# Reading the gate and up sums three weight chunks later, and turning units a block later, in an expert stage

## The chip, the cores and the metric

One core of a Trainium2 chip. The time is device microseconds of one launch, first to last instruction of the program on that core. TensorE is called PE (its weight loads PEld), VectorE DVE, ScalarE ACT, GpSimd POOL, SyncE SP; SP issues the transfers.

## The reference

Two transformer blocks on 256 tokens of width 1024, all in float32. The change is in the second block's last part, a mixture of eight experts of which each token takes two:

```python
gates = jnp.sum(jax.nn.one_hot(top_idx, N_EXPERTS) * top_w[..., None], axis=-2)
for e in range(N_EXPERTS):      # h: 256 x 1024; wg, wu: 1024 x 3584; wd: 3584 x 1024
    out = out + gates[..., e:e + 1] * ((jax.nn.silu(h @ wg[e]) * (h @ wu[e])) @ wd[e])
```

## The kernel before

**Precision.** Float32 products are made of rounded halves: `split` (L373) lets ACT cast a value to a short float (the high half, L374) and DVE subtract that from the value (the low half, a `tensor_tensor`, recorded at L339). `mm3` (L446) then makes three matmuls: high by high, high by low, low by high. Every weight is split on the chip.

**Weights.** They come in chunks of 512 rows by 512 columns (1 MB), fetched by SP into a ring of raw buffers (`fetch`, L390). `chunk` (L418) splits a chunk in two steps of 1024 columns, so a chunk is two casts on ACT and two subtractions on DVE. Low and high halves lie in rings of six buffers each in this stage, two per chunk: a chunk's split needs the buffers of the chunk three before it, and so waits until PE has read those. SP fetches into a raw buffer when DVE's subtraction has released it.

**Experts.** They are put in an order by load. Four of the eight are small (up to 64 tokens), four large (up to 128). A large expert keeps the halves of its tokens in separate columns and uses `mm3`; a small one holds both halves side by side in one 128 wide operand and needs two matmuls where a large one needs three. `gather` and `gather_small` collect an expert's tokens by matmuls into a PSUM bank, ACT scales them from there; `scatter` brings results back; `place` prepares both.

**Blocks.** An expert's 3584 columns are seven blocks of 512. A block is six chunks: two for gate (1024 rows), two for up, two for down. The loop over `steps` in `moe` (L2054) first does four blocks of a large expert, then alternates one block of a small and one of a large expert (a pair), and ends with four small ones. The unit that a block makes (silu(gate) times up, turned so that its columns lie on partitions, and split) is multiplied by the down weights in the next step, so that the order of chunks is: gate, gate, up, up of this block, then down, down of the block before.

**Around the sums.** `up` (L2105) takes two PSUM banks of pool `pd`, makes the gate sum in one and the up sum in the other, and lets ACT read the gate sum in between (a large block: Silu into `g`, right behind the splits of the second gate chunk) or at the end (a small block: copy, L2128). `up_end` (L2138 for a small block's up sum, `tt` for a large one's product) reads the up sum behind the first down chunk's splits, and PE turns the result into a bank of pool `ps` at once. `end`, which splits the turned unit into `hu` (L2160 for a large block; Silu, product, cast and subtraction for a small one), is put into `mids[0]`, which the next block's `up` runs after its first gate chunk. `mids` are four lists of such work, one after each chunk of `up`; gathers, scatters and `place` go into lists 1 and 2. The pool `ps` has five banks here, four of them hold the down sums of the two experts in work, and `pd` three.

The order on each engine is the program's order as far as the language's scheduler leaves it; `issue_after(x)` puts what follows behind `x` on its engine.

Of the kernel before, what the change touches and what calls it, by code (L numbers as in the profile page):

```python
# [212 lines left out]
class K:  # L213
# [1840 lines left out]
    def moe(self, x, lg, rs):  # L2054
        A, nc = self.A, self.nc
# [13 lines left out]
        NE, NB = 8, 7  # L2069
        small = [r >= SMALL for r in SEQ]  # L2070
# [31 lines left out]

        def up(e, cb, mids):  # L2105
            XH, XL = state[e][1][0], state[e][1][-1]
            g, ps = self.med(), []
            for nm in ("moe_w_gate_2", "moe_w_up_2"):
                p = self.take("pd")
                ps.append(p)  # L2110
                for kh in (0, 4):
                    with self.scope():
                        args = (W(nm, e), kh * 128, 4, cb * 512, 512)
                        c = self.chunk(*args)
                        for k in range(4):
                            ks = slice((kh + k) * 128, (kh + k) * 128 + 128)
                            if small[e]:
                                for i in range(2):
                                    self.last_mm = self.mm(p, XH[:, ks], c[k][i], kh + k + i == 0, kh + k + i == 8, True)
                            else:  # L2120
                                self.mm3(p, XH[:, ks], XL[:, ks], c[k][0], c[k][1], kh + k == 0, kh + k == 7)
                    for f in mids.pop(0):
                        f()
                if not small[e] and nm == "moe_w_gate_2":
                    self.act(g, p, AF.Silu)
            if small[e]:
                with self.tc.issue_after(self.last_hi.ins):
                    nc.scalar.copy(g, ps[0])  # L2128
            return g, p


        def up_end(e, g, pu):
            hu = self.take("r", 0)
            p = self.take("ps", 0)
            if small[e]:
                gu = self.med()
                with self.tc.issue_after(self.last_hi.ins):
                    nc.scalar.copy(gu, pu)  # L2138
                for i, a in enumerate((g, gu)):
                    for k in range(4):  # L2140
                        self.mm(p[:, i * 256 + k * 64 : i * 256 + k * 64 + 64], a[:, k * 128 : k * 128 + 128], self.cst("ident2"))

                def end():
                    with self.scope():
                        h = self.med()
                        self.act(h[:, :256], p[:, :256], AF.Silu)
                        self.tt(h[:, 256:], p[:, 256:], h[:, :256], ALU.mult)
                        v = hu[:, :512].rearrange("p (k h s) -> p k h s", k=4, h=2)
                        self.split(h[:, 256:].rearrange("p (k s) -> p k s", k=4), v[:, :, 0], v[:, :, 1])
                    self.free(p)  # L2150
                return hu, end
            with self.scope():
                h = self.med()
                self.tt(h, pu, g, ALU.mult)
                for k in range(4):
                    self.tr(p[:, k * 128 : k * 128 + 128], h[:, k * 128 : k * 128 + 128])

            def end():
                with self.tc.issue_after(self.last_hi.ins):
                    self.last_hi = nc.scalar.copy(hu[:, :512], p)  # L2160
                with self.tc.issue_after(self.last_lo.ins):
                    self.tt(hu[:, 512:], p, hu[:, :512].bitcast(F32), ALU.subtract)
                self.free(p)
            return hu, end

        def down(e, cb, hu, half):
            hh, hl = hu[:, :512], hu[:, 512:]
            if cb == half == 0:
                state[e][2] = [self.take("ps", 0), self.take("ps", 0)]
            acc = state[e][2]  # L2170
            with self.scope():
                c = self.chunk(W("moe_w_down_2", e), cb * 512, 4, half * 512, 512)
                for k in range(4):
                    ks = slice(k * 128, k * 128 + 128)
                    first, last = cb == 0 and k == 0, cb == NB - 1 and k == 3
                    if small[e]:
                        self.mm(acc[half], hh[:, ks], c[k][0], first, False)
                        self.last_mm = self.mm(acc[half], hh[:, ks], c[k][1], False, last)
                    else:
                        self.mm3(acc[half], hh[:, ks], hl[:, ks], c[k][0], c[k][1], first, last)  # L2180
            if half:
                self.free(hu)
# [18 lines left out]
        prev, mids = None, [[] for _ in range(4)]  # L2201
        for e, cb in steps:
            with self.scope():
                gp = up(e, cb, mids)
                mids = [[] for _ in range(4)]
                if cb == NB - 1:
                    self.free(*state[e][1])
                if prev:
                    down(*prev, 0)
                hu, end = up_end(e, *gp)  # L2210
                mids[0].append(end)
            if prev:
                for i, f in zip((1, 2), down(*prev, 1) or []):
                    mids[i].append(f)
            prev = (e, cb, hu)
# [24 lines left out]
            f()  # L2240
        for half in range(2):
            self.presplit(W("moe_w_down_2", NE - 1), (NB - 1) * 512, 4, half * 512, 512)
        self.q["pd"].append(self.q["ps"].popleft())
        self.overflow(x, gate, pos, scaled, ad, add, PP[0], cap)
        down(*prev, 0)
        for f in down(*prev, 1):
            f()
        for t in range(2):
            with self.scope():
                r = self.rms_of(t)  # L2250
# [62 lines left out]
```

## Time and profile before

| | |
|---|---|
| runs shown | 2153.07, 2149.79, 2152.31 us, median 2152.31 |
| profiled execution | 2151.22 us, its span 2149.4 us |
| PE busy | 2066.2 us, 96% of the span |
| DVE busy | 1841.5 us, 86% |
| ACT busy | 1325.3 us, 62% |
| read from HBM | 606.75 MB |

Matmuls overlap in the pipeline and their ends are modelled, so a busy PE need not be at its limit. What a wait costs is read from the stretch in which it lies: an engine's idle time is given with what ended it, and idle time of an engine that nothing waits for costs nothing.

### The profile page before, as it was taken

How to read it: one execution, taken by the hardware profiler on the slowest of the kernel's cores; microseconds unless marked ns; L12 is line 12 of the kernel's file. 1: busy time of each engine (PE TensorE's matmuls, PEld its weight loads, DVE VectorE, ACT ScalarE, POOL GpSimd, SP SyncE). 2: the span in 40 equal slices, each digit the busy share in tenths (PEclk: the TensorE clock that was granted, in tenths of full speed). 3: DMA queues.
4: the chain of work that ended last, by engine and by line, in shares of the span. 5: the costliest groups of instructions: out<-in, count | busy, mean ns of one | idle time of the engine just before them, and what ended most of it. 6: DMA issues, size and time to landing. Idle time of an engine off the chain costs nothing. (4 is left out here: it accounts for less than half of the span.)

```text
span 2149.4 us, 31135 instructions
## 1 busy us (share of the span) xinstructions
PE 2066.2 (96%) x11593; PEld 1706.1 (79%) x11593; DVE 1841.5 (86%) x2669; ACT 1325.3 (62%) x1857; POOL 2.1 (0%) x6
## 2 busy tenths in 40 slices
PE   6999999999999999999999999999999999999997
PEld 5987888889988878998997887777777777777765
DVE  6888985898888868888787999998998899998997
ACT  4544354454445435444765887777787778777775
POOL 0000000000000000000000000000000000000000
PEclk9999999999999999999999999999999999999997
DMA  7546767878843527885465899998999899998993
GB/s 306 192 165 214 264 219 255 298 296 303 302 160 117 150 100 262 310 342 212 139 253 188 329 400 368 356 387 321 391 343 377 348 365 377 355 383 322 386 371 140
DMA packets 99997, 610.70 MB, mean 284 GB/s; under 512 B 19156, under 2 KB 24061, under 8 KB 27773
## 3 DMA queue, kind: packets, MB, share of 16 engines
q1 hardware_dynamic: 99836, 608.64, 75.7%
q8 instruction: 92, 1.51, 0.3%
q14 instruction: 69, 0.56, 0.1%
HBM read 606.75 MB, written 3.42 MB: 284 GB/s over the span
## 5 line engine op out<-in xcount | busy, mean ns | idle before, releaser
L354 PE MATMUL pd<-k 128*128 128x512 f32 (+2 forms) x7408 | 1447.2, 349 | 37.8 <-DVE k L339 26.6
L339 DVE TENSOR_TENSOR k<-k,k 128x1024 fp32r<-128x1024 f32 (+2 forms) x1149 | 1229.8, 1112 | 184.4 <-ACT k L374 180.9
L354 PEld LDWEIGHTS pd<-k 128*128 128x128 f32 (+1 forms) x7408 | 1139.1, 190 | 269.3 <-DVE k L339 104.0
L374 ACT CAST k<-k 128x1024 fp32r<-128x1024 f32 (+2 forms) x1131 | 1039.6, 977 | 362.9 <-PE pd L354 184.6
L354 PE MATMUL ps<-k 128*128 128x512 f32 (+8 forms) x3031 | 576.2, 343 | 13.4 <-DVE k L339 3.8
L354 PEld LDWEIGHTS ps<-k 128*128 128x128 f32 (+4 forms) x3031 | 431.6, 179 | 112.1 <-DVE k L339 18.2
L348 DVE SCALAR_TENSOR_TENSOR k<-k,k 128x512 f32<-128x512 f32 (+1 forms) x257 | 188.3, 735 | 2.1 <-ACT k L351 0.2
L351 ACT ACTIVATE k<-pd 128x256 f32<-128x256 f32 (+1 forms) x125 | 57.2, 481 | 101.4 <-PE pd L354 98.5
L351 ACT ACTIVATE k<-k 128x256 f32<-128x256 f32 (+8 forms) x142 | 69.0, 500 | 79.3 <-DVE k L339 41.7
L339 DVE TENSOR_TENSOR k<-k 128x512 f32<-128x512 f32 (+13 forms) x277 | 93.6, 355 | 17.3 <-ACT k L351 12.4
L354 PEld LDWEIGHTS ps<-k,k 128*128 128x128 f32 x526 | 77.0, 199 | 12.4 <-DVE k L348 3.4
L339 DVE TENSOR_TENSOR k<-ps,k 128x512 fp32r<-128x512 f32 (+5 forms) x99 | 56.8, 579 | 24.8 <-PE ps L354 8.7
L354 PE MATMUL ps<-k,k 128*128 128x64 f32 (+3 forms) x526 | 75.0, 269 | 2.9 <-DVE k L348 2.9
L357 PE MATMUL ps<-k,k 128*128 128x128 f32 (+1 forms) x396 | 60.8, 278 | 16.7 <-DVE k L343 15.8
L357 PEld LDWEIGHTS ps<-k,k 128*128 128x128 f32 (+1 forms) x396 | 47.9, 143 | 30.5 <-DVE k L343 18.5
L339 DVE TENSOR_TENSOR k<-pd,k 128x512 f32<-128x512 f32 (+4 forms) x108 | 59.8, 568 | 12.5 <-PE pd L354 6.5
L351 ACT ACTIVATE k<-ps,k 128x128 f32<-128x128 f32 (+2 forms) x100 | 36.6, 446 | 42.8 <-DVE k L348 26.7
L348 DVE SCALAR_TENSOR_TENSOR k<-pd,k,k 128x255 f32<-128x255 f32 (+2 forms) x96 | 43.1, 474 | 4.4 <-ACT k L351 4.0
L2138 ACT COPY k<-pd 128x512 f32<-128x512 f32 x28 | 16.4, 586 | 48.2 <-PE pd L354 47.9
L345 DVE TENSOR_SCALAR k<-ps,k 128x128 f32<-128x128 f32 (+1 forms) x90 | 32.4, 405 | 10.5 <-PE ps L354 6.9
L348 DVE SCALAR_TENSOR_TENSOR k<-k 128x256 f32<-128x256 f32 (+7 forms) x121 | 36.9, 312 | 2.8 <-ACT k L351 1.1
L351 ACT ACTIVATE k<-ps 128x256 f32<-128x256 f32 (+2 forms) x30 | 12.4, 420 | 35.3 <-PE ps L354 35.3
(95 smaller groups left out, 416.1 us busy)
## 6 DMA issues: line engine op xcount, KB each, us to landing
k<-in_moe_w_up_dram SPq DMA_DIRECT2D x112, 1024.0 KB, 7.0
k<-in_moe_w_gate_dram SPq DMA_DIRECT2D x112, 1024.0 KB, 7.1
k<-in_moe_w_down_dram SPq DMA_DIRECT2D x112, 1024.0 KB, 7.2
k<-in_ada_w_dram SPq DMA_DIRECT2D x48, 1024.0 KB, 5.3
k<-in_w_in_dram SPq DMA_DIRECT2D x44, 1024.0 KB, 6.1
k<-in_w_ff_dram SPq DMA_DIRECT2D x32, 1024.0 KB, 6.0
k<-in_w_ada_dram SPq DMA_DIRECT2D x24, 1024.0 KB, 6.7
k<-in_cd_w_in_dram SPq DMA_DIRECT2D x14, 1024.0 KB, 4.9
```

The costliest lines, as they stand in the source:

```text
L339: return self.nc.vector.tensor_tensor(o, a, b, op=op)
L345: self.nc.vector.tensor_scalar(o, a, s1, s2, op0=op0, op1=op1)
L348: self.nc.vector.scalar_tensor_tensor(o, a, s, b, op0=op0, op1=op1)
L351: return self.nc.scalar.activation(o, a, f, **kw)
L354: return self.nc.tensor.matmul(o, l, r, start=start, stop=stop, skip_group_check=skip)
L357: return self.nc.tensor.transpose(o, i, self.ident[: i.shape[0], : i.shape[0]])
L374: self.last_hi = self.nc.scalar.copy(hi, src)
L2138: nc.scalar.copy(gu, pu)
```

## The change

Instructions, their shapes and their number stay as they are. What moves:

- `up` no longer reads its sums. `gate_out` (the Silu or the copy of the gate sum) runs behind the splits of the first down chunk, which is the third chunk after the gate sum's last.
- `up_out` (copy of a small block's up sum, product of a large one's) goes to `mids[0]` of the next block, behind the splits of its first gate chunk, again three chunks after.
- `turn` goes to `mids[1]` of the next block and takes a `pd` bank, not one of `ps`.
- `end`, the split of the turned unit, runs in `down` behind the splits of the first down chunk, right ahead of the matmuls that read it. The last block's unit is split behind the last weights.

```diff
         def up(e, cb, mids):
-            g, ps = self.med(), []
+            ps = []
...
-                if not small[e] and nm == "moe_w_gate_2":
-                    self.act(g, p, AF.Silu)
-            if small[e]:
-                with self.tc.issue_after(self.last_hi.ins):
-                    nc.scalar.copy(g, ps[0])
-            return g, p
+            return ps
+        def gate_out(e, b):
+            b["g"] = self.take("ms", 0)
+            with self.tc.issue_after(self.last_hi.ins):
+                if small[e]:
+                    nc.scalar.copy(b["g"], b["ps"][0])
+                else:
+                    self.act(b["g"], b["ps"][0], AF.Silu)
+            self.free(b["ps"][0])
+        def up_out(e, b):
+            b["h"] = self.take("ms", 0)
             if small[e]:
                 with self.tc.issue_after(self.last_hi.ins):
+                    nc.scalar.copy(b["h"], b["ps"][1])
+            else:
+                with self.tc.issue_after(self.last_lo.ins):
+                    self.tt(b["h"], b["ps"][1], b["g"], ALU.mult)
+            self.free(b["ps"][1])
-        def up_end(e, g, pu):
-            hu = self.take("r", 0)
-            p = self.take("ps", 0)
...
+        def turn(e, b):
+            p = b["p"] = self.take("pd", 0)
...
+        def end(e, b):
+            p, hu = b["p"], self.take("r", 0)
+            hi, lo = self.last_hi.ins, self.last_lo.ins
...
-        def down(e, cb, hu, half):
+        def down(e, cb, b, half, after=()):
...
                 c = self.chunk(W("moe_w_down_2", e), cb * 512, 4, half * 512, 512)
+                for f in after:
+                    f()
+                hh, hl = b["hu"][:, :512], b["hu"][:, 512:]
...
             with self.scope():
-                gp = up(e, cb, mids)
-                mids = [[] for _ in range(4)]
-                if cb == NB - 1:
-                    self.free(*state[e][1])
-                if prev:
-                    down(*prev, 0)
-                hu, end = up_end(e, *gp)
-                mids[0].append(end)
+                b = {"ps": up(e, cb, mids)}
+            mids = [[] for _ in range(4)]
+            if cb == NB - 1:
+                self.free(*state[e][1])
+            if prev:
+                down(*prev, 0, [lambda: end(prev[0], prev[2]), lambda: gate_out(e, b)])
+            else:
+                gate_out(e, b)
+            mids[0].append(lambda e=e, b=b: up_out(e, b))
+            mids[1].append(lambda e=e, b=b: turn(e, b))
...
         for half in range(2):
             self.presplit(W("moe_w_down_2", NE - 1), (NB - 1) * 512, 4, half * 512, 512)
+        end(prev[0], prev[2])
```

In the rows of the built order below, `k_64` are the split halves, `k_63` other buffers, `k_65` the identity or scales, `pd_..` and `ps_..` PSUM banks; L374 is the cast of a split, L354 a matmul, L357 a transposition.

ACT in a pair of blocks before, from the split of a large unit (L2160) to the next one: the small block's gate sum (L2128) and up sum (L2138), a turned small unit (128x256), the large gate sum (L351 from `pd_68`).

```order
L2160 CAST k_64<-ps_71 128x512
L374 CAST k_64<-k_63 128x1024 x6
L2128 COPY k_63<-pd_69 128x512
L374 CAST k_64<-k_63 128x1024 x2
L2138 COPY k_63<-pd_67 128x512
L374 CAST k_64<-k_63 128x1024 x2
L351 ACTIVATE k_63<-ps_71 128x256
L374 CAST k_64<-k_63 128x1024 x2
L374 CAST k_64<-k_63 128x4x64
L374 CAST k_64<-k_63 128x1024 x4
L351 ACTIVATE k_63<-pd_68 128x512
L374 CAST k_64<-k_63 128x1024 x8
```

The same after the change, where L2174 splits the large unit, L2131 and L2141 read the small block's gate and up sums:

```order
L2174 CAST k_64<-pd_68 128x512
L2131 COPY k_63<-pd_69 128x512
L374 CAST k_64<-k_63 128x1024 x4
L2141 COPY k_63<-pd_67 128x512
L374 CAST k_64<-k_63 128x1024 x8
L351 ACTIVATE k_63<-pd_69 128x256
L374 CAST k_64<-k_63 128x1024
L374 CAST k_64<-k_63 128x4x64
L351 ACTIVATE k_63<-pd_68 128x512
L374 CAST k_64<-k_63 128x1024 x11
```

Each reader of a sum stood right behind the casts of that sum or two casts later; now six casts lie between.

PE in a pair before, from a large block's up sum (`pd_67`): down of a small unit in two parts (`ps_73`, `pd_66`) with the large unit's four transpositions between, then a small block's gate and up sums, the small unit's turning (128x64) and the down of the large unit (`ps_72`).

```order
L354 MATMUL pd_67<-k_64 128x512 x24
L354 MATMUL ps_73<-k_64 128x512 x8
L357 MATMUL ps_71<-k_65,k_63 128x128 x4
L354 MATMUL pd_66<-k_64 128x512 x8
L354 MATMUL pd_68<-k_64 128x512 x16
L354 MATMUL pd_69<-k_64 128x512 x13
L354 MATMUL ps_71<-k_65,k_63 128x64 x2
L354 MATMUL pd_69<-k_64 128x512 x3
L354 MATMUL ps_71<-k_65,k_63 128x64
L354 MATMUL ps_72<-k_64 128x512
L354 MATMUL ps_71<-k_65,k_63 128x64
L354 MATMUL ps_72<-k_64 128x512 x11
```

And after the change, from a small block's gate sum (`pd_69`) to the next down of a small unit (`pd_66`, `ps_71`):

```order
L354 MATMUL pd_69<-k_64 128x512 x16
L357 MATMUL pd_68<-k_65,k_63 128x128 x4
L354 MATMUL pd_67<-k_64 128x512 x16
L354 MATMUL ps_70<-k_64 128x512 x2
L354 MATMUL pd_69<-k_65,k_63 128x64 x4
L354 MATMUL ps_70<-k_64 128x512 x10
L354 MATMUL ps_73<-k_64 128x512 x12
L354 MATMUL pd_68<-k_64 128x512 x24
L354 MATMUL pd_69<-k_65,k_63 128x64 x4
L354 MATMUL pd_67<-k_64 128x512 x24
L354 MATMUL pd_66<-k_64 128x512 x8
L354 MATMUL ps_71<-k_64 128x512 x8
```

The large unit's transpositions now stand between the next block's gate and up sums, 24 to 40 matmuls later, and the small unit's in two fours, one as soon as its gate part is read and one a block later.

The gather of a small expert, PE's part before: sixteen narrow matmuls into `ps_71` spread over a large block's gate sum (`pd_67`).

```order
L354 MATMUL ps_70<-k_64 128x512 x12
L354 MATMUL pd_67<-k_64 128x512
L354 MATMUL ps_71<-k_63 128x64 x4
L354 MATMUL pd_67<-k_64 128x512 x12
L354 MATMUL ps_71<-k_63 128x64 x4
L354 MATMUL pd_67<-k_64 128x512 x11
L354 MATMUL ps_71<-k_63 128x64 x8
L354 MATMUL pd_68<-k_64 128x512 x19
```

PE's part after, spread over the up sum (`pd_67`) of the small block ahead:

```order
L354 MATMUL pd_69<-k_64 128x512 x3
L354 MATMUL pd_67<-k_64 128x512
L354 MATMUL ps_72<-k_63 128x64
L354 MATMUL pd_67<-k_64 128x512 x4
L354 MATMUL ps_72<-k_63 128x64 x2
L354 MATMUL pd_67<-k_64 128x512 x3
L354 MATMUL ps_72<-k_63 128x64
L354 MATMUL pd_67<-k_64 128x512
L354 MATMUL ps_72<-k_63 128x64 x8
L354 MATMUL pd_67<-k_64 128x512 x4
L354 MATMUL ps_72<-k_63 128x64 x2
L354 MATMUL pd_67<-k_64 128x512 x3
```

ACT's part before, the eight scalings that read that bank, right behind the large Silu:

```order
L374 CAST k_64<-k_63 128x1024 x4
L351 ACTIVATE k_63<-pd_67 128x512
L351 ACTIVATE k_63<-ps_71,k_65 128x64 x8
L374 CAST k_64<-k_63 128x1024
L374 CAST k_64<-k_63 128x8x64
L374 CAST k_64<-k_63 128x1024 x7
```

and after, a block later than PE's part:

```order
L351 ACTIVATE k_63<-pd_68 128x512
L374 CAST k_64<-k_63 128x1024
L351 ACTIVATE k_63<-ps_70,k_65 128x64 x2
L374 CAST k_64<-k_63 128x1024 x2
L351 ACTIVATE k_63<-ps_70,k_65 128x64 x4
L374 CAST k_64<-k_63 128x1024 x2
L351 ACTIVATE k_63<-ps_70,k_65 128x64 x2
L374 CAST k_64<-k_63 128x8x64
```

PE's matmuls of the gather moved ahead by half a block and ACT's readers moved back and apart.

## Rows read from the trace of the kernel before

**Rows 1.** Table by stretches: us, busy of each engine, clock, DMA share, GB/s

```profile
1240.00:2130.00 890.00, 859.43 (x3871) 651.93 (x3870) 804.52 (x813) 690.42 (x842) 0.00 (x0) 1.00 0.93 359
1468.10:1711.80 243.70, 235.83 (x1065) 178.44 (x1064) 218.25 (x223) 188.41 (x231) 0.00 (x0) 1.00 0.94 363
1520.30:1552.60 32.30, 31.98 (x144) 24.20 (x143) 29.42 (x28) 25.87 (x32) 0.00 (x0) 1.00 0.99 391
1250.00:1300.00 50.00, 49.69 (x228) 39.69 (x226) 47.67 (x48) 40.89 (x48) 0.00 (x0) 1.00 1.00 405
2131.00:2149.40 18.40, 5.76 (x11) 3.15 (x11) 8.87 (x16) 5.91 (x14) 0.00 (x0) 0.54 0.16 59
```

**Rows 2.** Waits, 1240 to 2130: us in total, times, longest

```profile
DVE k L339 <- ACT k L374: 71.7, 67, 6.7
ACT k L351 <- PE pd L354: 57.6, 30, 3.8
ACT k L2138 <- PE pd L354: 47.9, 24, 3.7
ACT k L351 <- PE ps L354: 39.1, 28, 3.6
...
ACT k L2128 <- PE pd L354: 18.0, 15, 1.9
...
ACT k L374 <- PE ps L354: 12.8, 10, 1.6
DVE k L339 <- ACT k L351: 9.1, 17, 0.5
```

**Rows 3.** ACT in order of time, one pair: start, length, instruction, idle before

```profile
1527.20 0.60 ACT L351 ACTIVATE k<-pd 128x512 f32<-128x512 f32 x1 [1.93 <-PE pd L354]
...
1547.23 0.59 ACT L2138 COPY k<-pd 128x512 f32<-128x512 f32 x1 [0.88 <-PE pd L354]
...
1551.27 0.39 ACT L351 ACTIVATE k<-pd 128x256 f32<-128x256 f32 x1 [1.55 <-PE pd L354]
```

**Rows 4.** DVE in order of time, the same pair

```profile
1528.76 4.63 DVE L339 TENSOR_TENSOR k<-k,k 128x1024 fp32r<-128x1024 f32 x4 [1.27 <-ACT k L374]
...
1538.45 0.68 DVE L339 TENSOR_TENSOR k<-pd,k 128x512 fp32r<-128x512 f32 x1
1539.05 9.16 DVE L339 TENSOR_TENSOR k<-k,k 128x1024 fp32r<-128x1024 f32 x8
1548.79 2.36 DVE L339 TENSOR_TENSOR k<-k,k 128x1024 fp32r<-128x1024 f32 x2 [0.58 <-ACT k L374]
1551.69 0.42 DVE L339 TENSOR_TENSOR k<-pd,k 128x256 f32<-128x256 f32 x1 [0.53 <-ACT k L351]
1552.62 1.23 DVE L339 TENSOR_TENSOR k<-k,k 128x1024 fp32r<-128x1024 f32 x1 [0.51 <-ACT k L374]
```

**Rows 5.** PE and its weight loads in order of time, the same pair

```profile
1521.30 8.38 PEld L354 LDWEIGHTS pd<-k 128*128 128x128 f32 x37
...
1550.23 1.00 PE L354 MATMUL pd<-k,k 128*128 128x64 f32 x8
```

**Rows 6.** ACT and DVE in order of time around two gathers

```profile
1578.07 1.83 DVE L339 TENSOR_TENSOR k<-k,k 128x1024 fp32r<-128x1024 f32 x2 [2.03 <-ACT k L374]
...
1700.31 2.47 ACT L351 ACTIVATE k<-ps,k 128x64 f32<-128x64 f32 x8 [1.14 <-PE ps L354]
...
1703.75 2.96 DVE L339 TENSOR_TENSOR k<-k,k 128x1024 fp32r<-128x1024 f32 x3 [6.72 <-ACT k L374]
```

**Rows 7.** SP's queue: its waits from 1240 to 2130, then its issues from 1174

```profile
SPq L393 <- DVE k L339: 710.8, 303, 9.1
...
1174.26 0.33 SPq L393 DMA_DIRECT2D k<-in_moe_w_up_dram  x1
1179.06 3.20 SPq L393 DMA_DIRECT2D k<-in_moe_w_down_dram  x2
```

**Rows 8.** Weight loads in order of time behind the branch near the end

```profile
2134.08 0.93 PEld L354 LDWEIGHTS ps<-k 128*128 128x128 f32 x3 [3.86 <-issue]
```

More of the change, by code (lines that the diff above doesn't have):

```diff
@@ L2106, in up @@
             XH, XL = state[e][1][0], state[e][1][-1]
-            g, ps = self.med(), []
+            ps = []
             for nm in ("moe_w_gate_2", "moe_w_up_2"):
-                p = self.take("pd")
+                p = self.take("pd", 0)
                 ps.append(p)
@@ L2112, in up @@
                     with self.scope():
-                        args = (W(nm, e), kh * 128, 4, cb * 512, 512)
-                        c = self.chunk(*args)
+                        c = self.chunk(W(nm, e), kh * 128, 4, cb * 512, 512)
                         for k in range(4):
@@ L2135, in up_end @@
             if small[e]:
-                gu = self.med()
-                with self.tc.issue_after(self.last_hi.ins):
-                    nc.scalar.copy(gu, pu)
-                for i, a in enumerate((g, gu)):
+                for i, a in enumerate((b["g"], b["h"])):
                     for k in range(4):
                         self.mm(p[:, i * 256 + k * 64 : i * 256 + k * 64 + 64], a[:, k * 128 : k * 128 + 128], self.cst("ident2"))
-                def end():
-                    with self.scope():
-                        h = self.med()
+            else:
+                for k in range(4):
+                    self.tr(p[:, k * 128 : k * 128 + 128], b["h"][:, k * 128 : k * 128 + 128])
@@ L2146, in end @@
+            self.free(b["g"], b["h"])
+        def end(e, b):
+            p, hu = b["p"], self.take("r", 0)
+            hi, lo = self.last_hi.ins, self.last_lo.ins
+            if small[e]:
+                with self.scope():
+                    h = self.med()
+                    with self.tc.issue_after(hi):
                         self.act(h[:, :256], p[:, :256], AF.Silu)
+                    with self.tc.issue_after(lo):
                         self.tt(h[:, 256:], p[:, 256:], h[:, :256], ALU.mult)
-                        v = hu[:, :512].rearrange("p (k h s) -> p k h s", k=4, h=2)
@@ L2149, in end @@
[L2149 to L2159, printed above, removed]
+                    v = hu[:, :512].rearrange("p (k h s) -> p k h s", k=4, h=2)
@@ L2160, in end @@
+                    self.split(h[:, 256:].rearrange("p (k s) -> p k s", k=4), v[:, :, 0], v[:, :, 1])
+            else:
+                with self.tc.issue_after(hi):
                     self.last_hi = nc.scalar.copy(hu[:, :512], p)
-                with self.tc.issue_after(self.last_lo.ins):
+                with self.tc.issue_after(lo):
                     self.tt(hu[:, 512:], p, hu[:, :512].bitcast(F32), ALU.subtract)
-                self.free(p)
-            return hu, end
-        def down(e, cb, hu, half):
-            hh, hl = hu[:, :512], hu[:, 512:]
+            self.free(p)
@@ L2168, in down @@
+            b["hu"] = hu
+        def down(e, cb, b, half, after=()):
             if cb == half == 0:
@@ L2181, in down @@
             if half:
-                self.free(hu)
+                self.free(b["hu"])
             if cb == NB - 1 and half:
@@ L2203, in moe @@
             with self.scope():
-                gp = up(e, cb, mids)
-                mids = [[] for _ in range(4)]
-                if cb == NB - 1:
-                    self.free(*state[e][1])
-                if prev:
-                    down(*prev, 0)
-                hu, end = up_end(e, *gp)
-                mids[0].append(end)
+                b = {"ps": up(e, cb, mids)}
[4 more added lines that the diff above has]
+                down(*prev, 0, [lambda: end(prev[0], prev[2]), lambda: gate_out(e, b)])
+            else:
+                gate_out(e, b)
+            mids[0].append(lambda e=e, b=b: up_out(e, b))
+            mids[1].append(lambda e=e, b=b: turn(e, b))
             if prev:
@@ L2214, in moe @@
                     mids[i].append(f)
-            prev = (e, cb, hu)
+            prev = (e, cb, b)
             if (e, cb) == (0, 0):
```

## The prediction

> **What bounds the kernel now.** I read the table by stretches first, then the waits, then one pair of blocks on each engine. The stage that the change touches runs from about 1168 to 2130 us; I take 1240 to 2130, 890 us of it, in which blocks of large and small experts alternate.
>
> In the table by stretches [rows 1] the reader should see three loads close together. PE reads 859 us of 890, but its weight loads only 652. DVE reads 804.5, so it is idle 85.5 us. The DMA engines are at 0.93 and move 359 GB/s. In the waits of the same stretch [rows 2] DVE's idle time has one cause: 71.7 us behind an ACT cast (L374) and 9.1 us behind an ACT activation (L351), 81 of 85.5. ACT is not slow (690 us busy); it waits for PE: 57.6 + 47.9 + 39.1 + 18.0 = 163 us, nearly all in instructions that read a gate or up sum, or the turned unit of a small expert. So the chain is: ACT stands in front of a sum that PE has not finished, the casts queued behind it on ACT are late, DVE (the low halves of the splits) runs dry, PE runs dry after that.
>
> One undisturbed pair, 1520.3 to 1552.6, shows it instruction by instruction. ACT waits 1.93 us for a large gate sum, 0.88 us for a small up sum and 1.55 us for a turned small unit [rows 3]. DVE idles 1.27 us after the first, 0.58 us after the second, 0.53 and 0.51 us around the third [rows 4]: together 2.89 us, and the stretch has 32.30 - 29.42 = 2.88. The pair is DVE's work plus what ACT withholds from it.
>
> **PE has room.** 37 weight loads of a run without waits take 8.38 us [rows 5], 0.2265 us each. A large block has 72 wide matmuls, a small one 48: 27.2 us, and both turnings at most 2 x 1.00 us [rows 5], so 29.2 us against 32.3.
>
> **The change, part by part.** No instruction is added or removed; all is order.
>
> *Readers of sums.* In the order ACT now has six casts, those of three later chunks, between the casts that a sum needs and the instruction that reads it. Splits run at most three chunks ahead of PE (six buffers, two per chunk), so when ACT has cast the third chunk after a sum, PE must be through with that sum. The waits of rows 3 should go to zero, and with them 2.89 us of DVE idle in a pair. Over two experts (14 blocks, 1468.1 to 1711.8) DVE idles 243.7 - 218.25 = 25.4 us [rows 1]. Two idles are of another kind, the gathers of the next experts: 6.72 and 2.03 us [rows 6]. That leaves 16.7; five undisturbed pairs give 14.5. I take 15. The stretch has 890 / 243.7 = 3.65 such cycles: **55 us**, bounds 53 and 61.
>
> *Gathers.* They also wait for PE: 1.14 us and more before eight activations of 2.47 us, during which no cast is issued [rows 6]. The order shows PE's sixteen gather matmuls moved ahead, out of the large gate sum into the small up sum, since the turned unit no longer holds that PSUM bank; ACT's eight activations now stand in groups of two and four between casts. The wait should go, the activations' own time stays. Of 3.65 x 8.75 = 32 us I take half, **16 us**, bounds 0 and 32.
>
> *The small unit's chain.* Silu (ACT), product (DVE), cast (ACT), subtraction (DVE) is still four hops. Without the wait for PE the 0.53 us goes; the cast may still hold ACT until DVE comes to the product, and DVE then lacks the next cast. No row shows this alone; the nearest are 0.53 and 0.51 us. Bounds 0 and 1.04 per pair; I take 0.4, for 26 pairs **-10 us** (0 to -27).
>
> *Scatters.* ACT casts a finished down sum while PE is barely done with it: 12.8 us in 10 waits now [rows 2]. An ACT that is held less is further ahead of PE and waits longer here. Bounds: nothing, or twice as long, all of it passed to DVE (-26); I take **-8 us**.
>
> *The unit just before its use.* This is the new wait. The split of the turned unit now follows the low halves of the down chunk that needs it, so PE can't start down before two low halves (9.16 / 8 = 1.145 us each) and 0.68 us more [rows 4], 2.97 us. Queued behind that matmul on PE is the whole next block. Does PE come early enough to wait? From the moment a large unit is ready PE has 24 down and 48 gate and up matmuls and a turning, 72 x 0.2265 + 1.0 = 17.3 us, before it needs the small unit. DVE needs for that one 13 low halves and 0.42 us twice, 15.7 us. PE is 1.6 us late and does not wait. From there to the next large unit PE has 48 x 0.2265 + 1.0 = 11.9 us, DVE the other 11 low halves and 2 x 0.68, 14.0 us: PE waits 14.0 - 11.9 - 1.6 = 0.5 us. DVE, which sets the pace, loses nothing: PE's lag of under 3 us is about one chunk of the three that the buffers hold. Cost 0, cover: that lag.
>
> *SP's queue.* The loads of the experts' order move ahead of one up transfer, which was issued at 1174.26, with the next issues from 1179.06 [rows 7]: it comes at most 4.8 us later. SP waits 710.8 us of 890 for DVE to release a raw buffer [rows 7], so loaded buffers stand in reserve: 0.
>
> *The DMA lid.* Faster readers ask for more. The undisturbed pair already moves 391 GB/s at 0.99, and 50 us reach 405 at 1.00 [rows 1]. At 391 the 890 us would be 890 x 359 / 391 = 817, so no more than 73 us can be had here, 101 at 405. The Trainium skill sets the lid lower ("DMA: Bandwidth & Descriptors", Where 436 GB/s comes from): for transfers between HBM and SBUF the core's share of HBM, about 358 GB/s, is what binds. By that rule there would be nothing to gain; the trace differs, by its two rows above 358. My sum lies below the 73 us, but with two limits a few per cent apart some time is lost between them: **-5 us** (0 to -15).
>
> *The tail.* The last unit is now split after the last weights, so the last down's 16 matmuls, 13 of which ran before the branch, come after it. Before the branch's end PE stood 3.86 us [rows 8]; now it reaches the branch sooner and can pass it while DVE still works. Then 13 x 0.2265 = 2.9 us, or twice that, since the granted clock of the last stretch is 0.54, about the lower of its two levels [rows 1]. I bound this part by 4 us gained and 6 lost and take **-1 us**.
>
> Sum: 55 + 16 - 10 - 8 - 5 - 1 = 47. The profiled execution took 2151.22 us, 1.1 under the median 2152.31; 2151.2 - 47 = 2104, and for a median I say **2105**.
>
> **Rivals.**
> 1. *Only part is recovered.* Gathers stay as dear (0), the small chain keeps its whole 1.04 us (-27), scatters and tail as above: 55 - 27 - 8 - 1 = 19, so **2132**. For it: ACT is in order and every hop to DVE and back remains. Against: the waits on PE that began those idles are gone.
> 2. *All of DVE's idle goes,* and the DMA engines become the bound: 73 us, **2078**. For it: the average rate is 359, far under 405. Against: the four hops and the eight activations.
> 3. *Slower: PE waits for the unit at every down.* If PE came to down at DVE's heels each time, it would stand 2 x 2.97 = 5.9 us a pair; its pair of 29.2 would be 35.1, 2.8 over today's 32.3, and 26 pairs make it 73 us slower, **2224**. The point from which it decides is 3.1 us of standing per pair (29.2 + 3.1 = 32.3); I count 0.5. For it: in small blocks PE waits for low halves at every step now, so its lag is small there. Against: a large block's matmuls outlast DVE's work on it, and the down follows.
> 4. *No change: the transfers are at their limit already.* If 359 GB/s were all that this stage can be given, DVE would wait for landings where it waits for casts, **2151**. Against: 391 and 405 in the rows above, and SP waiting for buffers, not DVE for data. It is what the rule on the share of HBM, in the Trainium skill's page named above, would give.
>
> **How the numbers follow.** Forecast 0.60, rival 1 0.17, rival 2 0.11, rival 3 0.07, rival 4 0.05. About 0.2% (4 us) is what a measurement of this kernel can tell from no change. Faster: the first three cases, 0.88; within 0.2%: 0.05; slower: 0.07. The likeliest time is 2105. The low end is rival 2's 2078, the high end lies just over rival 1, 2137; what is left out is rivals 3 and 4 and the edges of the others.
>
> **What would show it.** Right, step by step: the waits of ACT for gate and up sums (L2131, L2141, the large Silu) fall from 163 to under 30 us over the stage; DVE's idle behind ACT from 81 to about 35; an undisturbed pair takes 30 to 31.5 us; DMA share near 0.97, with more than 375 GB/s; ACT's gather activations no longer preceded by a wait. Wrong: PE's wait for the split unit (the cast and the subtraction before down) over 3 us a pair, as in rival 3; ACT waiting for landings at an unchanged 359 GB/s, rival 4; DVE's idle moved to the product and cast of the small unit at 1 us a pair, rival 1.

## The result and the profile after

The changed kernel takes **2117.37 us** (median of 4 runs, 2116.02 to 2120.37) against 2151.05 (4 runs of the kernel before on the same chip): ratio 0.9846 [0.9829, 0.9863], 33.7 us faster. The forecast was 2105 with a range of 2078 to 2137: the sign held, and the mechanism for the readers of gate and up sums; the gain was forecast at 47. The profiled execution took 2116.02 us, with a span of 2114.2.

The table by stretches of the kernel after (us; busy of PE, PE's weight loads, DVE, ACT and POOL; clock; DMA share; GB/s) answers to [rows 1]: the stage, a cycle of two experts, an undisturbed pair of blocks, two blocks of that cycle that are not undisturbed with the block behind the second, and the end.

```profile
1240.00:2095.00 855.00, 819.80 (x3858) 671.03 (x3856) 804.71 (x813) 701.21 (x842) 0.00 (x0) 0.99 0.95 373
1457.10:1691.70 234.60, 225.40 (x1066) 183.62 (x1065) 218.53 (x223) 191.45 (x231) 0.00 (x0) 0.99 0.97 377
1959.90:1989.60 29.70, 29.57 (x141) 24.61 (x140) 29.26 (x29) 26.42 (x30) 0.00 (x0) 1.00 1.01 420
1505.90:1525.40 19.50, 18.23 (x94) 15.30 (x93) 14.51 (x16) 11.79 (x15) 0.00 (x0) 1.00 0.91 360
1540.20:1560.70 20.50, 18.21 (x93) 15.18 (x92) 16.14 (x20) 14.17 (x19) 0.00 (x0) 1.00 0.95 364
1560.70:1576.40 15.70, 14.89 (x67) 10.97 (x66) 15.70 (x17) 13.27 (x16) 0.00 (x0) 1.00 0.95 357
2095.00:2114.20 19.20, 9.35 (x24) 6.20 (x24) 8.92 (x17) 5.94 (x14) 0.00 (x0) 0.68 0.15 56
```

DVE's work in the stage is the same to a fifth of a microsecond, so the gain is DVE's idle time: 855 - 804.7 = 50 us where 85.5 stood. The pair went from 32.3 to 29.7 us, with PE, DVE and the DMA engines all full. The cycle went only from 243.7 to 234.6: two of its fourteen blocks take 19.5 and 20.5 us where the same two took 15.9 each before. (The block behind the second went from 19.1 to 15.7, so these two blocks together went from 35.0 to 36.2.)

The waits of the same stretch (engine and line, what it waited for, us in total, times, longest) answer to [rows 2]:

```profile
ACT k L374 <- PE pd L354: 54.2, 123, 2.1
DVE k L339 <- ACT k L374: 37.1, 55, 4.6
ACT k L374 <- DVE k L339: 30.0, 17, 3.8
ACT k L374 <- PE ps L354: 29.4, 45, 2.1
...
PE ps L354 <- DVE k L339: 17.0, 18, 2.4
ACT k L1998 <- PE ps L357: 13.9, 5, 5.8
PE pd L354 <- DVE k L339: 10.3, 10, 2.4
ACT k L374 <- issue: 9.1, 5, 2.3
...
ACT k L1998 <- PE pd L357: 5.8, 1, 5.8
...
ACT k L351 <- PE pd L354: 3.4, 5, 1.2
```

ACT's 163 us before gate sums, up sums and turned units are down to this 3.4. What ACT now waits for, 123 and 45 times, is PE freeing a buffer of the splits, mostly 0.30 us at a time: it is as far ahead as the buffers let it be. And it waits for things it hardly waited for before: the copy of the slots' transposition in `slots` (L1998) 19.7 us, longest 5.8, against 8.0; a small unit's product on DVE 30.0 against 5.9.

ACT in order of time in the kernel after (start, length, instruction, idle before it and its releaser) at the first of the two long blocks:

```profile
1510.11 1.06 ACT L374 CAST k<-k 128x1024 fp32r<-128x1024 f32 x1 [0.30 <-PE pd L354]
1511.47 1.06 ACT L374 CAST k<-k 128x1024 fp32r<-128x1024 f32 x1 [0.30 <-PE pd L354]
1518.30 0.38 ACT L1998 CAST k<-pd 128x256 fp32r<-128x256 f32 x1 [5.77 <-PE pd L357]
1518.57 2.00 ACT L374 CAST k<-k 128x1024 fp32r<-128x1024 f32 x2
```

and DVE there:

```profile
1504.80 10.30 DVE L339 TENSOR_TENSOR k<-k,k 128x1024 fp32r<-128x1024 f32 x9
1519.65 2.36 DVE L339 TENSOR_TENSOR k<-k,k 128x1024 fp32r<-128x1024 f32 x2 [4.55 <-ACT k L374]
```

It is the old pattern in a new place: ACT stands 5.77 us before a young sum, the casts behind it are late, DVE is idle 4.55 us. The second long block holds the gather of a large expert. On ACT:

```profile
1543.26 8.22 ACT L374 CAST k<-k 128x512 fp32r<-128x512 f32 x9 [2.33 <-issue]
...
1555.71 0.40 ACT L374 CAST k<-k 128x256 fp32r<-128x256 f32 x1 [3.01 <-DVE k L339]
```

and on DVE:

```profile
1544.87 6.90 DVE L339 TENSOR_TENSOR k<-k,k 128x1024 fp32r<-128x1024 f32 x6 [2.30 <-ACT k L374]
1552.38 2.96 DVE L339 TENSOR_TENSOR k<-k,k 128x512 fp32r<-128x512 f32 x3 [0.61 <-PE pd L354]
...
1557.12 0.73 DVE L345 TENSOR_SCALAR k<-pd,k 128x128 f32<-128x128 f32 x2 [1.45 <-PE pd L354]
```

The first cast of the gathered tokens waits 2.33 us for something the profile doesn't name (run 6 comes back to it); the second half's operations on DVE wait 1.45 us for PE's gather matmuls. DVE loses 4.4 us in this block.

### The profile page after: what moved, and what is told of

It is laid out like the page before. It is cut to its first block, busy times and chain, and to the rows that moved or that the text cites. A ratio compares the mean times of both kernels' runs of the same rounds, so it can differ in the third digit from the quotient of the medians.

```text
span 2114.2 us, 31293 instructions
## 1 busy us (share of the span) xinstructions
PE 2027.3 (96%) x11593; PEld 1726.4 (82%) x11593; DVE 1842.3 (87%) x2669; ACT 1336.2 (63%) x1857; POOL 2.1 (0%) x6
## 4 chain that ended last, share of the span: by engine, by line
PE 79%; DVE 12%; ACT 4%; issue 3%; DMA 2%; SPq 0%; DVEq 0%; ACTq 0%
PE pd L354 54%; PE ps L354 23%; DVE k L339 8%; ACT k L374 2%; DVE k L348 2%; ACT k L351 1%; DMA k<-in_w_in_dram 1%; PE pd L357 1%; PE ps L357 1%; DVE k L343 0%; DVE k L345 0%; DMA k<-in_w_out_dram 0%; DMA k<-in_x_dram 0%; DVE k L922 0%; ACT k L2131 0%
## 5 line engine op out<-in xcount | busy, mean ns | idle before, releaser
L354 PE MATMUL pd<-k 128*128 128x512 f32 (+2 forms) x7414 | 1410.5, 346 | 23.6 <-DVE k L339 14.8
L374 ACT CAST k<-k 128x1024 fp32r<-128x1024 f32 (+2 forms) x1131 | 1055.3, 976 | 471.8 <-PE pd L354 234.6
L354 PEld LDWEIGHTS pd<-k 128*128 128x128 f32 (+1 forms) x7414 | 1150.3, 189 | 200.8 <-DVE k L339 29.9
L354 PE MATMUL ps<-k 128*128 128x512 f32 (+8 forms) x3025 | 565.3, 344 | 25.2 <-DVE k L339 19.9
L354 PEld LDWEIGHTS ps<-k 128*128 128x128 f32 (+4 forms) x3025 | 441.8, 181 | 121.5 <-DVE k L339 30.2
L348 DVE SCALAR_TENSOR_TENSOR k<-k,k 128x512 f32<-128x512 f32 (+1 forms) x257 | 188.5, 735 | 2.1 <-ACT k L351 0.3
L351 ACT ACTIVATE k<-k 128x256 f32<-128x256 f32 (+8 forms) x142 | 69.0, 500 | 78.8 <-DVE k L339 41.8
L339 DVE TENSOR_TENSOR k<-pd,k 128x512 f32<-128x512 f32 (+4 forms) x155 | 85.8, 564 | 11.4 <-PE pd L354 6.1
L351 ACT ACTIVATE k<-pd 128x256 f32<-128x256 f32 (+1 forms) x148 | 65.7, 463 | 46.6 <-PE pd L354 43.8
L354 PE MATMUL pd<-k,k 128*128 128x64 f32 (+1 forms) x472 | 69.3, 286 | 4.9 <-ACT k L2131 4.9
L354 PEld LDWEIGHTS pd<-k,k 128*128 128x128 f32 x472 | 63.0, 192 | 11.4 <-ACT k L2131 6.2
L357 PE MATMUL ps<-k,k 128*128 128x128 f32 x302 | 47.2, 280 | 16.8 <-DVE k L343 15.8
L351 ACT ACTIVATE k<-ps,k 128x128 f32<-128x128 f32 (+2 forms) x100 | 37.4, 448 | 35.1 <-DVE k L348 28.0
L357 PEld LDWEIGHTS ps<-k,k 128*128 128x128 f32 x302 | 36.4, 144 | 27.2 <-DVE k L343 18.5
L339 DVE TENSOR_TENSOR k<-ps,k 128x512 f32<-128x512 f32 (+5 forms) x52 | 30.8, 604 | 21.0 <-PE ps L354 12.2
L348 DVE SCALAR_TENSOR_TENSOR k<-pd,k,k 128x255 f32<-128x255 f32 (+2 forms) x96 | 43.1, 476 | 4.4 <-ACT k L351 4.0
L357 PE MATMUL pd<-k,k 128*128 128x128 f32 (+1 forms) x222 | 36.8, 280 | 4.9 <-DVE k L1346 4.9
L348 DVE SCALAR_TENSOR_TENSOR k<-k 128x256 f32<-128x256 f32 (+7 forms) x121 | 37.0, 313 | 3.0 <-ACT k L351 1.3
L357 PEld LDWEIGHTS pd<-k,k 128*128 128x128 f32 (+1 forms) x222 | 28.1, 143 | 11.7 <-DVE k L1346 5.2
```

The lines of the kernel that those rows point to most:

```text
L339: return self.nc.vector.tensor_tensor(o, a, b, op=op)
L348: self.nc.vector.scalar_tensor_tensor(o, a, s, b, op0=op0, op1=op1)
L351: return self.nc.scalar.activation(o, a, f, **kw)
L354: return self.nc.tensor.matmul(o, l, r, start=start, stop=stop, skip_group_check=skip)
L357: return self.nc.tensor.transpose(o, i, self.ident[: i.shape[0], : i.shape[0]])
L374: self.last_hi = self.nc.scalar.copy(hi, src)
```

## The experiments

All start from the changed kernel, and are compared with the kernel before, whose medians were 2150.45 to 2151.03. The theory: an instruction on ACT (or DVE) that reads a sum which PE has not finished stops an engine that runs in order, and everything behind it is late; moving such readers behind later splits is the whole gain, and what is left of it lies at the readers that the change did not move. The rivals stand in the expectations.

**1. The gate sum's reader back, the up sum's stays late.**

```diff
-                down(*prev, 0, [lambda: end(prev[0], prev[2]), lambda: gate_out(e, b)])
+                down(*prev, 0, [lambda: end(prev[0], prev[2])])
 # in up(), behind the second gate chunk (large) or behind both sums (small):
+                    gate_out(e, b)
```

> The change with one part undone: a large block's gate sum is read right behind the casts of its second gate chunk again, a small block's behind its up chunks; up sums, turning and the split of the unit stay as in the change. Theory A (DVE sets the pace and loses what ACT loses in front of unfinished sums): ACT waits again about 2 us per pair for the large gate sum, DVE idles 1.3 us behind it, 26 pairs: 25 to 35 us over the change, 2142 to 2152. Theory B (the gain came from the PSUM bank that turning no longer holds, so that gathers start early): within 5 us of the change's 2117.

Measured: 2159.46 us, ratio to before 1.0038 [1.0024, 1.0052], so 42 us over the change and slightly over the kernel before: more than theory A's 25 to 35, and far from theory B's 5. The waits of this run from 1240 to 2095:

```profile
ACT k L351 <- PE pd L354: 90.0, 25, 4.4
DVE k L339 <- ACT k L374: 78.5, 37, 4.5
```

This one early reader is enough to lose everything. ACT waits 3.6 us each time (90.0 / 25) where it waited 1.9 [rows 2]: with the other readers late it comes to the gate sum further ahead of PE than before; DVE's idle behind it is 78.5 against 71.7.

**2. The up sum's reader back to one chunk later.**

```diff
-                down(..., [..., lambda: gate_out(e, b)])
+                down(..., [..., lambda: gate_out(e, b), lambda: up_out(e, b)])
-            mids[0].append(lambda e=e, b=b: up_out(e, b))
```

> The change with another part undone: both up sums are read behind the first down chunk's splits, one chunk after the sum's last and not three. Theory A: ACT waits 1 to 2 us for each small up sum and DVE itself for each large one before its product, 0.6 us and up to 1.5 us of DVE idle per pair: 15 to 50 us over the change, 2132 to 2167. Theory B: within 5 us of 2117.

Measured: 2120.1 us, 0.9856 [0.9839, 0.9872]: the loss expected did not come, the interval overlaps that of the change. ACT's waits of this run from 1240 to 2095:

```profile
ACT k L2141 <- PE pd L354: 44.4, 20, 4.0
...
ACT k L374 <- PE pd L354: 25.3, 73, 2.1
...
ACT k L374 <- PE ps L354: 18.4, 33, 2.1
```

The copies of the small experts' up sums wait 44.4 us again, and the waits for buffers of the splits are 40 us less (43.7 against 83.6). DVE's idle behind ACT's casts is 38.1 us against 37.1. So here ACT would have stood anyway, which fits a wait of ACT being lost only where it uses up ACT's lead over DVE; no run tests that rule by itself.

**3. The slot copy in the next block.** The transpositions of `slots` stay, ACT's copy of them goes to the next block, behind the splits of its first gate chunk.

```diff
-            self.nc.scalar.copy(PG, p[:, :256])
+        def out():
+            with self.tc.issue_after(self.last_hi.ins):
+                self.nc.scalar.copy(PG, p[:, :256])
+            self.free(p)
+        return out
...
+            if late:
+                mids[0].append(late.pop())
```

> The change, and the rule of three chunks also for the copy of an expert's placement out of PSUM (L1998), which goes to the next block behind its first gate chunk. In the change ACT waits 19.7 us in six such copies, up to 5.8 us, where it waited 8.0 before. Theory A: that wait goes, and of DVE's idle 4.6 + 1.2 us per two experts: 15 to 20 us under the change, 2097 to 2102. Theory C (with ACT no longer held, PE or the transfers are the bound, and ACT's waits are free): at most 4 us under, 2113 or more.

Measured: 2111.61 us, 0.9823 [0.9807, 0.9840]: 5.8 us faster than the change, a third of what was expected and more than the rival allowed. The waits at the copy are gone and the block of 19.5 us takes 14.8; but the gathers' activations, which hardly waited in the changed kernel, now do, three times 5.0 us at a small expert's and twice 3.1 at a large one's:

```profile
ACT k L351 <- PE ps L354: 21.2, 5, 5.0
```

The wait had moved on to the next early reader.

**4. A unit's read-out one chunk earlier** (undoes a part of the change's delay, and takes away the new wait of PE just before down).

```diff
-                down(*prev, 0, [lambda: end(prev[0], prev[2]), lambda: gate_out(e, b)])
+                down(*prev, 0, [lambda: gate_out(e, b)])
+            mids[3].append(lambda e=e, b=b: end(e, b))
```

> Edit to the changed kernel: a unit's read-out (ACT copy, DVE subtract, or the small expert's activation and product) goes behind the last up chunk instead of behind the first down chunk, one chunk ahead of the matmuls that use it. The rest of the change stays. Theory A (the read-out just before its use is a real new wait: PE's sums ps waited 17.0 us for DVE in 1240 to 2095, and the weight loads ps 24.2): 5 to 12 us faster than the change, near 2108. Theory B (those waits are where PE has slack, and ACT would now meet the turned sum of a PE that is up to three chunks behind): same or up to 15 us slower, 2117 to 2132, with ACT waits for PE at the unit's copy or activation.

Measured: 2125.19 us, 0.9881 [0.9865, 0.9898]: 7.8 us slower than the change. PE's waits for DVE at the sums of down did halve, 8.4 us against 17.0, but ACT waits for unfinished sums again:

```profile
ACT k L351 <- PE pd L354: 22.5, 11, 3.9
```

Eight of the 11 are turned small units, 12.3 us together, up to 3.4 each; the other three, 10.2 us, are a large expert's gather, which waited 0.5 to 1.2 us in the changed kernel. Theory B holds: the late read-out is worth more than the wait it brings. The fourth part of the change, the later turning, was not undone by itself.

**5. Gathers' readers one chunk later as well** (on top of run 3). The matmuls of a gather stay where they are; the activations, DVE's operations and the split that read their sum run behind the next chunk.

```diff
                     for i, f in zip((1, 2), begin(n)):
-                        mids[i].append(f)
+                        hold = []
+                        mids[i].append(lambda f=f, hold=hold: hold.append(f()))
+                        mids[i + 1].append(lambda hold=hold: hold.pop()())
```

> On top of the run that puts the slot copy later (2111.6 us): the readers of the gathers' sums (the eight activations of a small expert, the four activations or four VectorE operations and the splits of a large one) go one chunk behind their matmuls. Theory A (ACT's waits for young sums are still what costs outside the undisturbed pairs: 5.0 us at a small expert's gather, 3.1 at a large one's, and DVE idle behind them, 8.9 us in one cycle of two experts): 10 to 30 us faster, 2082 to 2102. Theory B (PE has become the limit in the blocks with gathers as well; it was busy 19.80 of 19.80 us in that block, so that only its own idle time can be won, some 1.1 to 2.4 us in a place): 0 to 6 us faster, 2105 to 2112.

Measured: **2096.16 us**, 0.9752 [0.9735, 0.9769], 21.2 faster than the change and the fastest of these kernels that compute everything. Theory A holds. The table by stretches of this run: the cycle, the two blocks that were long with the block behind the second, and an undisturbed pair.

```profile
1451.30:1677.80 226.50, 221.46 (x1066) 183.05 (x1065) 217.56 (x222) 192.37 (x232) 0.00 (x0) 1.00 0.97 391
1500.50:1515.30 14.80, 14.80 (x72) 12.32 (x71) 14.36 (x15) 11.53 (x13) 0.00 (x0) 1.00 1.00 415
1530.20:1545.50 15.30, 15.30 (x75) 12.84 (x74) 14.60 (x16) 11.87 (x14) 0.00 (x0) 1.00 1.01 422
1545.50:1565.50 20.00, 18.63 (x101) 15.67 (x100) 17.69 (x21) 16.50 (x22) 0.00 (x0) 1.00 0.89 353
1938.30:1968.00 29.70, 29.60 (x141) 24.61 (x141) 29.30 (x29) 26.43 (x30) 0.00 (x0) 1.00 1.01 421
```

The two long blocks are now about as short as half an undisturbed pair, and that pair is the 29.7 us of the change. Part of the large gather's time has only moved one block on, from 15.7 to 20.0 us there, so that the two blocks together went from 36.2 to 35.3; over the cycle 8.1 us are won (234.6 to 226.5).

**6. The gathers' readers alone**, the slot copy as in the change.

> Edit to the changed kernel: the later gather readers alone; the slot copy stays where the change has it. The two late readings together gave 2096.2 us, the slot copy alone 2111.6, the change 2117.4. Theory I (each wait is lost on its own): 15 us faster than the change, 2099 to 2106. Theory S (what the gathers give back, ACT loses again at the slot copy, where it waits up to 5.8 us): 2107 to 2117.

Measured: 2101.33 us, 0.9772 [0.9756, 0.9788]: 16.0 faster than the change, so theory I. Gathers 16, slot copy 5 to 6, together 21. The casts' waits without a named releaser, 9.1 us in the change, are down to 1.1 here. A kernel with eleven buffers for split units instead of ten, meant to show whether those waits were for such a buffer, does not fit (211.6 kB a partition where 207.9 are left), so what they were for stays open.

**7. Scatters one chunk later too** (on top of run 5).

```diff
-                for i, f in zip((1, 2), down(*prev, 1) or []):
+                for i, f in zip((2, 3), down(*prev, 1) or []):
```

> On top of the later gather readers: both halves of a scatter start one chunk later. Theory A (ACT's 2.9 us wait at a scatter's split, 1.2 of it passed on to DVE, about four times in the window, is lost time): 3 to 8 us faster than the run with later gather readers. Theory B (PE is the limit there): within 2 us of it.

Measured: 2103.86 us, 0.9784 [0.9768, 0.9800]: 7.7 us *slower* than run 5, which neither theory had. The scatter's first wait stayed (1.21 us in this run, 1.20 in run 5). Its additions on VectorE (L348) moved. The first addition behind a scatter, in run 5:

```profile
1575.22 0.75 DVE L348 SCALAR_TENSOR_TENSOR k<-pd,k 128x512 f32<-128x512 f32 x1 [0.54 <-PE pd L354]
```

The same in this run, and two casts of ACT behind it:

```profile
1580.45 0.75 DVE L348 SCALAR_TENSOR_TENSOR k<-pd,k 128x512 f32<-128x512 f32 x1 [2.16 <-PE pd L354]
...
1585.86 0.41 ACT L374 CAST k<-k 128x256 fp32r<-128x256 f32 x1 [2.53 <-DVE k L339]
...
1590.20 1.04 ACT L374 CAST k<-k 128x1024 fp32r<-128x1024 f32 x1 [2.51 <-issue]
```

It is the pattern of the change once more, now on DVE: the addition waits 2.16 us for a sum of PE where it waited 0.54, and everything behind it on DVE is late. The block takes 20.4 us instead of 18.8, and so do the two other blocks with such a scatter, 4.8 us of the 8.4 between the two profiled spans. ACT's 2.53 us before the cast of the small unit's product are hardly new (2.31 in run 5). PE then waits 1.47 and 2.04 us for DVE in this block, where it waited 1.26 in run 5. The 2.51 us of ACT have no releaser in the profile. That the additions' place is the whole loss was not tested by itself.

**8. PE relieved.** In the large experts the product of the low half of the tokens, or of the unit, with the weights is left out (24 of 143 matmuls of a pair).

```diff
-  self.mm3(p, XH[:, ks], XL[:, ks], c[k][0], c[k][1], ...)      # and the same in down
+  self.mm2(p, XH[:, ks], XL[:, ks], c[k][0], c[k][1], ...)      # without sl * rh
```

> Edit to the changed kernel: the large experts leave out the product of the tokens' (or the unit's) low half with the weights, so 24 of 143 matmuls of a pair, 5 us of PE's 29.8; every split is still made, so VectorE keeps its 29.6 us in 30.0 and the bytes stay. The output is not the reference's. Theory P (in undisturbed pairs PE is the limit, and the waits for young sums elsewhere are there because PE is behind): 20 to 50 us faster than the change, 2067 to 2097. Theory V (VectorE paces just as tightly, PE's fullness is its shadow): pairs fall from 30.0 to 29.5 us at best, 2 to 15 us in all, 2102 to 2115.

Measured: 2088.11 us, 0.9708 [0.9692, 0.9724]: 29.3 us faster than the change, as theory P had it, but not for P's first reason. The undisturbed pair of this run:

```profile
1935.20:1964.80 29.60, 26.49 (x118) 20.98 (x118) 29.16 (x29) 25.52 (x31) 0.00 (x0) 0.96 1.00 413
```

PE has 3.1 us to spare and the pair takes 29.6 instead of 29.7. There VectorE paces as tightly as PE (theory V). What PE's relief gave lies elsewhere: by the table of blocks below, 7 us before the stage, 17 us from block 5 to 53, 3 to 4 us behind. DVE's idle behind ACT's casts falls to 26.7 us from 37.1; that this is because ACT waits for a PE that is less far behind is likely and not shown.

**9. PE and DVE relieved.** As 8 with another product left out in down, and the low halves of the large experts' down weights not made.

```diff
+                if not low:
+                    lo = self.last_hi = self.nc.scalar.copy(h, v[:, k : k + step])
...
+                        self.mm(acc[half], hh[:, ks], c[k][0], first, False)
+                        self.last_mm = self.mm(acc[half], hl[:, ks], c[k][0], False, last)
```

> Edit to the changed kernel: the large experts leave out one of three products everywhere (low half of the tokens times weights in gate and up, tokens times low half of the weights in down) and the low half of the down weights is not made, so the output is not the reference's. In an undisturbed pair this takes 24 of 143 matmuls from PE (29.8 to about 24.7 us) and four VectorE subtracts of 1.15 us (29.6 to about 25.0); ScalarE stays at 26.4 us and the bytes stay. Theory D (transfers at 420 GB/s are a lid of their own at 30.0 us a pair): pairs stay at 29.5 to 30 us; the total falls by under 20 us, to 2098 or above. Theory E (PE and DVE were the lid, the transfers only keep pace): pairs fall to 26.5 to 28 us and the total by 50 to 100 us, 2020 to 2067.

Measured: 2036.31 us, 0.9467 [0.9451, 0.9483], 81 us faster than the change: theory E. The stage of this run, and an undisturbed pair:

```profile
1240.00:2010.00 770.00, 697.87 (x3182) 549.94 (x3183) 673.50 (x696) 669.66 (x822) 0.00 (x0) 0.96 0.99 408
1887.00:1914.10 27.10, 25.10 (x117) 19.80 (x117) 24.84 (x24) 25.38 (x32) 0.00 (x0) 1.00 1.01 421
```

The pair falls from 29.7 to 27.1 us at the same share and rate, so the transfers were not the lid at 373 GB/s, nor what held the pair at 420. (A pair's 12 chunks of 1 MB would take an estimated 29.9 us at 421 GB/s, so this pair also used chunks that were loaded before.) At 408 GB/s over 770 us, with a share of 0.99, they are the fullest now; that they already bind here is not shown, for ACT waits only 1.5 us in all for a landing. No run relieves DVE alone, so how the gain divides between PE and DVE stays open.

## Why the prediction was right, and where it was off

The kernel's blocks can be compared one by one by where DVE starts the first low half of a block (us in each profiled span; an expert has seven blocks, so the 14 from 18 to 32 are a cycle of two experts):

| | before | change | 3: slot copy | 5: + gathers | 8: PE relieved |
|---|---|---|---|---|---|
| block 5 | 1244.1 | 1243.7 | 1241.7 | 1243.1 | 1236.6 |
| block 18 | 1468.1 | 1457.1 | 1455.3 | 1451.3 | 1446.0 |
| block 32 | 1711.8 | 1691.7 | 1688.4 | 1677.8 | 1673.2 |
| block 46 | 1955.4 | 1926.3 | 1919.6 | 1904.4 | 1901.4 |
| block 53 | 2072.3 | 2034.4 | 2027.6 | 2012.9 | 2009.9 |
| last split ends | 2130.5 | 2093.9 | 2087.8 | 2072.4 | 2066.5 |
| span ends | 2149.4 | 2114.2 | 2106.9 | 2092.8 | 2086.2 |

- **Readers of sums: right.** Blocks 46 to 53 have no gather or slot copy: 116.9 us before, 108.1 after, 2.5 us a pair where 2.89 less 0.4 for the small unit's chain was forecast. The pair of 29.7 is just below the 30 to 31.5 named, and DVE's idle behind ACT's casts fell to 37.1 where about 35 was named. Had all 24 pairs of blocks 5 to 53 won 2.5 us, it would be 24 x 2.5 = 60 us; the forecast's 55 - 10 = 45 left out what DVE idles at the gathers.
- **Gathers: the step that failed.** "The wait should go, the activations' own time stays. Of 3.65 x 8.75 = 32 us I take half, **16 us**." The wait at a small expert's activations did go, and 0.5 to 1.2 us are left at a large one's. But behind these the split waited for something unnamed and DVE's half for a young sum: 4.4 us of DVE in one block. By blocks, a cycle's two with a large expert's gather went from 35.0 to 36.2 us, where an undisturbed pair won 2.5; its four with a small expert's went from 71.3 to 64.7, where two such pairs won 5.0. Blocks 5 to 53 won 828.2 - 790.7 = 37.5 us of the 60. The gain was there to be had: run 6 shows 16.0 us by moving these readers too. And the 6.72 us [rows 6] that were all put down to the gather were not its own: in the kernel before, ACT's longer wait in front of it was for the large gate sum, a reader of the first step's kind.

```profile
1698.58 0.60 ACT L351 ACTIVATE k<-pd 128x512 f32<-128x512 f32 x1 [3.77 <-PE pd L354]
```

- **The slot copy: missing from the sum.** The step on scatters names the mechanism, an ACT that is held less is further ahead of PE and waits longer, and gives it up to twice the wait; it was not asked of every remaining reader. At the slot copy the wait went from 8.0 to 19.7 us; run 3 shows 5.8 us of time for it. One such copy stands in the very pair that the prediction read, where ACT waited 2.06 us and DVE lost nothing by it:

```profile
1539.81 0.37 ACT L1998 CAST k<-pd 128x256 fp32r<-128x256 f32 x1 [2.06 <-PE pd L357]
```

  With both moved (run 5) blocks 5 to 53 win 828.2 - 769.8 = 58.4 us. That this nearly makes up the 60 holds for the sum, not block by block: four of the cycle's blocks still take 18.8 to 20.0 us.
- **Scatters: sign right, too small** (-8). By blocks, the two of a cycle with a scatter went from 37.8 to 39.0 us where a pair won 2.5: 3.7 us a cycle, an estimate of 14 over the stage, inside the bounds of 0 and 26. Run 7, which moved them, lost time.
- **The unit just before its use: cost 0 in undisturbed pairs, as forecast.** PE is idle 29.70 - 29.57 = 0.13 us in one. Elsewhere PE waits for DVE there, 17.0 us in 18 waits against 3.5 before, but run 4 shows that the alternative costs 7.8 us more.
- **PE has room: a narrow yes.** 29.2 us of work were counted, 29.57 are busy in 29.70. DVE (29.26) and the transfers (1.01) are as full. The prediction saw DVE alone at the end. Run 8 shows that with PE relieved DVE holds the pair within 0.1 us of where it was, run 9 the gain when both give way; that PE alone would hold it is read from its busy time.
- **The DMA lid: not contradicted, not measured by itself** (-5). The mean rate came to 373 GB/s, not "more than 375", and the share to 0.95 rather than 0.97; the two long blocks have 360 and 364 GB/s, the undisturbed pair 420.
- **The tail: sign right** (-1). From the last split to the end 20.3 us against 18.9, 1.4 lost; the blocks from 53 to the last split lost another 1.3 (59.5 against 58.2).
- **The rivals.** The result lies between the forecast and rival 1, but rival 1's reasons held only in part: gathers gave little, as it says, but an undisturbed pair lost 29.70 - 29.26 = 0.44 us of DVE in all, not 1.04 to the small unit's chain. Rival 3 did not happen (0.13 us of PE's standing in a pair, not 5.9). Rival 2's 2078 was not reached: DVE still idled 50 us. Rival 4 fell with the pair at 420 GB/s.
- **Together, partly luck.** Forecast: 45 for the sums less the small chain, 16 - 8 = 8 for gathers and scatters, -5 and -1, so 47. Measured between the profiled spans, by blocks: 0.4 before block 5, 60 from the pairs' gain, 60 - 37.5 = 22.5 lost again at slot copies, gathers and scatters, 2.7 lost at the end, so 35.2. The first term was some 15 us too small, the second some 30 too large, and these errors partly cancel.

## What to carry to other kernels

When an engine that runs in order is freed of one wait, it runs further ahead and every remaining reader of a fresh result can cost more: list all such readers on that engine, not only those that top the table of waits, and move them together. One left in place can return the whole gain (run 1) or cost nothing that shows (run 2); the last ones gave more than half as much again as the change (run 5), and a move can put other work in front of a fresh sum (run 7). Before pricing a gain, count every engine's work in an undisturbed stretch: where three loads come out within 3 per cent of each other and of the time, order alone has little more to give there.

## What had not been expected of the hardware

A single core drew 420 GB/s over undisturbed pairs (DMA share 1.01) and 408 over 770 us on end (run 9). The page of the Trainium skill that the prediction weighed ("DMA: Bandwidth & Descriptors", Where 436 GB/s comes from) puts the bound for HBM to SBUF at about 358; another page of the Trainium skill, "Perfetto Trace Analysis" (Roofline), says that with one core of a pair active about 120% of that is the practical ceiling, an estimate of 430 GB/s. The traces agree with the second: 420 lies above 358 and below 430.

Of the granted clock: the end of the program, where PE has little to do, ran at 0.68 after and 0.54 before [rows 1]. In run 8, with PE at 26.49 us of 29.60, the stretch was granted 0.96, and in run 9, with PE at 697.87 of 770, also 0.96; the change's pair, with PE at 29.57 of 29.70, had 1.00. An undisturbed pair of run 9, with PE at 25.10 of 27.10, had 1.00 too; what makes the difference is not shown.
